# Seven-product pairs with seeded PSUM: two vector additions for five, fixed PSUM regions and mixed values kept in DRAM

## The chip, the cores and the metric

The kernel runs on one NeuronCore of one Trainium2 chip. The metric is the time of one execution in microseconds (us) of the device. In the profile PE is the matmul engine (PEld its weight loads), DVE the vector engine, ACT the scalar (activation) engine, POOL the general one, and SP the engine that issues DMAs (SPq is its queue). SBUF is the core's working memory, PSUM the memory that matmuls write and accumulate in; a PSUM bank holds 512 fp32 values in each of 128 partitions.

## What is computed

One layer of a decoder trunk for 1,032 tokens (a prompt of 1,024 and 8 samples of one token), all of width 1,024:

```python
xn = rmsnorm(h, pre_g)
u, v, z_a, x_b, z_b, g_a, g_b = split(xn @ w_in)              # seven blocks of 1024 columns
u, vn = gelu(u), layernorm(gelu(v), ln_g, ln_b)
y_a = u * (tril(w_s) @ vn + b_s) * silu(z_a)                  # w_s within chunks of 128 tokens
y_b = (pool(x_b) @ blockdiag(w_pool)) * scale * silu(z_b)     # trailing windows 2, 4, 8, 16
m = sigmoid(g_a) * (y_a @ w_pa) + sigmoid(g_b) * (y_b @ w_pb)
h = h + rmsnorm(m @ w_out, post_g)
h = h + rmsnorm(sigmoid(rmsnorm(h) @ w_pg) * (p @ w_ple), ple_out_g)
```

Besides `h` the kernel returns the last chunk's `vn` and the last rows of `x_b`.

## The kernel before, in words

**Seven products for eight.** Each of the large matmuls is split into 2 x 2 blocks and done with seven block products, P1 to P7, in place of eight (the scheme of Strassen in Winograd's form). It works on a *pair*: two blocks of 128 output features at a time (`pairs_of`, four pairs to a block of 1,024). The output of a pair is features first: 128 partitions are features, the columns are tokens, 512 in the first half and 520 (`WIDE`: 512 and the 8 samples) in the second. So the products are narrow (512 columns) or wide (520, as two matmuls of 260). fp32 values are cut into a high and a low part of a rounded type (names ending in `h` and `l`), and three terms (high x high, high x low, low x high) are added up in PSUM: a narrow product is 12 matmuls of 512 columns, a wide one 24 of 260 (`product`).

**Operands.** The 1,024 x 1,032 activations lie in `big`. `Operand.combine` turns their quarters, in place, into the sums B11, B21, B22, T1 to T4 that the products need, and `Operand.cut` cuts each into high and low parts (`xB11h`, `xT3l`, ...), which are kept for all pairs of a stage. On the weights' side `Weights` fetches a pair's 1,024 x 256 raw weights (`gbraw`: two DMAs of 512 KB), forms sums (`gbs`) on DVE, rounds (`gbw`) on ACT, and takes the low part on DVE, all pair by pair.

**A pair's products** (`strassen`, L691). Order P1, P6, P2, P7, P5, P4, P3 (the planner below may move neighbours). `Step` holds for each product what prepares its weights, the matmuls, and `evacuate`, what is done when PSUM holds the result. ACT copies P1 from PSUM to `u` in SBUF (L706, and 8 zero columns from `none`); then DVE makes five additions that read PSUM: u = P6 + u, u7 = P7 + u, and P5 + u7, P4 + u7 and P3 + u, which go to the output tile (`user.summed`). P2 accumulates on P1's bank and is handed on directly (`user.direct`). `User` and its children (`V`, `Gate`, `U`, `ZA`, `XB`, `ZB`, `Merge`, `MergeB`) apply gelu, silu or sigmoid and multiply. The first three v pairs, `EDGES`, have an order of their own (`EDGE`).

**Stages.** Start: loads, transposes of x (`x_half`, PSUM tiles `pst`), the embedding p @ w_ple (`embed`, PSUM tiles `e`), norms, and the first v pairs, interleaved by a list, `SCRIPT`. Then the pairs of v, g_a, u with z_a, x_b with z_b (and after each the pooled matmul, `mixes`), g_b, w_pa, w_pb; then w_out and the gate w_pg, which work tokens first (`strassen_within`), with norms in between, and the outputs. The spatial mixing (`spatial`, L1118) writes its result into `big`, and `ZA.done` (L1198) reads it there. The sums of the windows (`XB.window`) use `big` as scratch as well, each block of a pair its own two rows of it.

**What sets the order.** Nothing is issued as the code stands. Every call goes to a `Planner` (L99), which records operations with a due time from a cost model of its own, and plays them engine by engine from one line (L374, so that every operation of the profile bears that line). `PUSH` moves due times forward (or back, where it is negative) by kind. It also hands out 46 slots of SBUF (`SLOTS`) and, of the three PSUM regions `acc` of two banks each, whichever is free (`region`, L425), under names `pst`, `acc`, `accm`, `acct`, `e`; two more banks serve `bank`. An engine takes its instructions strictly in the order so written, and an instruction waits for its inputs and for its output's place.

Of the kernel before, what the change touches and what calls it, by code (L numbers as in the profile page):

```python
# [14 lines left out]
P = 128  # L15
# [16 lines left out]
PUSH = {'hs': -4.0, 'norm': -5.0, 'half': 0.0, 'cut': -1.0, 'e': 2.0, 'we': -2.0, 'vw': -9.0, 'p': 3.0}  # L32
# [8 lines left out]
OS, GS = 5, 12  # L41
WINDOWS = (2, 4, 8, 16)
# [339 lines left out]
def hybrid_step(  # L382
# [12 lines left out]
    accp = ctx.enter_context(tc.tile_pool(name="accp", bufs=3, space=bass.MemoryType.PSUM))  # L395
    bankp = ctx.enter_context(tc.tile_pool(name="bankp", bufs=2, space=bass.MemoryType.PSUM))
    plan = Planner(nc, SLOTS, {"acc": 3, "bank": 2})
# [64 lines left out]
    big = cpool.tile([P, NB, T], F32, tag="big", name="big")  # L462

# [35 lines left out]
    class Operand:  # L499
# [5 lines left out]
                    "T1": (0, 1), "T2": (0, 0), "T3": (1, 1), "T4": (1, 0)}  # L505
# [9 lines left out]
        def cut(self, what):  # L515
            i, j = self.QUARTERS[what]
            for kk in range(2):
                hi, lo = self.new(what, kk)
                if what == "T2":
                    split(quarter(kk, 0), hi[:, :, :HALF], lo[:, :, :HALF])  # L520
                    split(quarter(2 + kk, 1)[:, :, HALF:], hi[:, :, HALF:], lo[:, :, HALF:])
                else:
                    split(quarter(2 * i + kk, j), hi, lo)

        def combine(self, what):
            for kk in range(2):
                b11, b12, b21, b22 = (quarter(2 * i + kk, j) for i in range(2) for j in range(2))
                if what == "T3":
                    sub(b22, b22, b12)
                elif what == "T1":  # L530
                    sub(b12[:, :, :HALF], b12[:, :, :HALF], b11)
                elif what == "T2":
                    add(b11, b22[:, :, :HALF], b11)
                else:
                    sub(b21, b21, b11)
# [80 lines left out]
    class Features:  # L616

        new = staticmethod(lambda: region("acc"))
# [16 lines left out]
    class Tokens:  # L635

        new = staticmethod(lambda: region("acct")[:, 0])
# [53 lines left out]
    def strassen(weights, operand, user, form=Features, order=None):  # L691
# [41 lines left out]
        for p, a, b, r in sorted(plan, key=lambda x: order.index(x[0])) if order else plan:  # L733
            def run(p=p, a=a, b=b, r=r):
                new = r not in at
                if new:
                    at[r] = form.new()
                product(form, at[r], weights.ready[a], operand, b, new, True, not new)

            steps.append(Step(lambda a=a: weights.prepare(a), run, lambda p=p: evacuate(p)))  # L740
        steps[0].loads = lambda: (weights.fetch(), user.loads())
# [223 lines left out]
    def x_half(j, kps):  # L965

        for kp in kps:
            two = region("pst") if kp != 1 else None
            ps = [bank("pst") if two is None else two[:, kk] for kk in range(2)]
            for i in range(4):  # L970
                plan.apart()
                for kk in range(2):
                    k = 2 * kp + kk
                    nc.tensor.transpose(ps[kk][:, i * P : (i + 1) * P],
                                        xts[4 * j + i][:, k * P : (k + 1) * P], ident)
            out = quarter(kp, j)[:, :, :HALF]
            for kk in range(2):
                o, i, gain = out[:, kk], ps[kk], col(0, 2 * kp + kk)
                if SIDES[4 * j + kp]:
                    nc.scalar.activation(out=o, in_=i, func=AF.Copy, scale=gain)  # L980
                else:
                    nc.vector.tensor_scalar_mul(o, i, gain)
# [22 lines left out]
    vtok = lambda t: sv if t == S else big[:, t, :D]  # L1005
# [112 lines left out]
    def spatial(t):  # L1118

        vh, vl = lnv.pop(("cut", t))  # L1120
        for h2 in range(0, NB, 2):
            ps = bank("mix").rearrange("p (h c t) -> p h c t", h=2, c=2)
            for i in range(2):
                h = h2 + i
                w = lnt["wst"][h // 4][:, h % 4]
                c = slice(h * P, (h + 1) * P)
                nc.tensor.matmul(ps[:, i], vh[:, c], w, start=True, stop=False)
                nc.tensor.matmul(ps[:, i, 0], vl[:, c], w[:, 0], start=False, stop=True)
            o = big[:, t, h2 * P : (h2 + 2) * P].rearrange("p (h t) -> p h t", h=2)
            nc.scalar.activation(out=o, in_=ps[:, :, 0], func=AF.Copy)  # L1130
            add(o, ps[:, :, 1], o)

# [17 lines left out]
    kept["h"] = dram.tile([T, D], F32, tag="h", name="h")  # L1150
    kept["e"] = dram.tile([T, D], F32, tag="e", name="e")
# [68 lines left out]
    def pool_state():  # L1220
        dma(big[: NS * POOL_BUF, 7, :D], state.rearrange("b r d -> (b r) d"))
# [11 lines left out]
    state_sb, tail = big[:, 7, :D], big[:, 6, :D]  # L1233
# [11 lines left out]
    class XB(User):  # L1245
# [10 lines left out]
        def window(self, i):  # L1256
# [4 lines left out]
            s, free = x, [big[:, 2 * i, :], big[:, 2 * i + 1, :]]  # L1261
# [23 lines left out]
    def mixes(g):  # L1285
# [12 lines left out]
        for m in range(2):  # L1298
            def run(m=m):
                for j in range(2):  # L1300
                    ps = held[m, j] = region("accm")
# [55 lines left out]
    for i, (w, u) in enumerate(pairs_of(V0, V, "v")):  # L1357
        vsteps.append(strassen(w, xop, u, order=EDGE if i < EDGES else None))
        vusers.append(u)
    gasteps = [strassen(w, xop, u) for w, u in pairs_of(GA0, Gate, "ga")]  # L1360
    usteps = []
    zausers = []
    for (w, u), (wz, z) in zip(pairs_of(U0, U, "u"), pairs_of(ZA0, ZA, "za")):
        usteps.append((strassen(w, xop, u), strassen(wz, xop, z)))
        zausers.append(z)
    bsteps, xusers = [], []
    for g, ((w, u), (wz, z)) in enumerate(zip(pairs_of(XB0, XB, "xb"), pairs_of(ZB0, ZB, "zb"))):
        bsteps.append((strassen(w, xop, u), strassen(wz, xop, z), mixes(g)))
        xusers.append(u)
    gbsteps = [strassen(w, xop, u) for w, u in pairs_of(GB0, Gate, "gb")]  # L1370

    flat, c = big.rearrange("p b t -> p (b t)"), [T + 4 * w for w in (0, HALF, HALF + WIDE, HALF + 2 * WIDE)]
# [4 lines left out]
    pasteps = [strassen(Weights(merged(w_pa, i), "pa"), yaop, u)  # L1377
               for i, u in enumerate(pausers)]
    pbusers = [MergeB(i, "gb") for i in range(NPAIR)]
    pbsteps = [strassen(Weights(merged(w_pb, i), "pb"), ybop, u)  # L1380
# [6 lines left out]
    for g, (x, z, mix) in enumerate(bsteps):  # L1387
        steps += x[:3] + late + x[3:] + z
        late = mix
    steps += gbsteps[0][:3] + late + gbsteps[0][3:]  # L1390
# [26 lines left out]
    for g, u in enumerate(xusers):  # L1417
# [3 lines left out]
        follow = bsteps[g + 1][0] if g + 1 < NPAIR else gbsteps[0]  # L1421
# [7 lines left out]
        at(follow[5], store)  # L1429
# [9 lines left out]
    PARTS = ("B11", "T2", "B21", "T3", "T4", "T1", "B22")  # L1439
# [257 lines left out]
    def embed(q, n):  # L1697

        hi, lo = pcut[q // 2]
        ps = e_ps[q, n] = region("e")  # L1700
# [28 lines left out]
    def begin():  # L1729
# [68 lines left out]
        def combines():  # L1798
            for what in ("T3", "T1", "T2"):
                xop.combine(what)  # L1800
            xop.cut("T2")
            xop.combine("T4")
            for what in ("T3", "T1", "T4"):
# [58 lines left out]
```

## Time and profile before

| | |
|---|---|
| time, three runs | 976.70, 977.16, 977.18 us (median 977.16) |
| span of the profiled execution | 975.6 us; the median of the runs is 1.6 us above it |
| PE, PEld, DVE, ACT, POOL busy | 963.1, 855.9, 813.4, 497.9, 74.2 us |
| matmuls | 6,037 records |
| moved by SP's queue | 177.43 MB |
| granted clock of PE, mean | 0.998 |

A row of the timeline gives start and duration in us, the engine, the line, the operation, output<-input by the names of the program without their numbers, and shapes as partitions x columns; `x4` is four in a row, and a bracket tells how long the engine had been idle before and what ended that. A row of a group gives busy us and the mean in ns behind the first bar, idle time before it behind the second. A row of waits reads: who <- for whom: us in total, times, longest.

### The profile page before, as it was taken

How to read it: one execution, taken by the hardware profiler on the slowest of the kernel's cores; microseconds unless marked ns; L12 is line 12 of the kernel's file. 1: busy time of each engine (PE TensorE's matmuls, PEld its weight loads, DVE VectorE, ACT ScalarE, POOL GpSimd, SP SyncE). 2: the span in 40 equal slices, each digit the busy share in tenths (PEclk: the TensorE clock that was granted, in tenths of full speed). 3: DMA queues.
4: the chain of work that ended last, by engine and by line, in shares of the span. 5: the costliest groups of instructions: out<-in, count | busy, mean ns of one | idle time of the engine just before them, and what ended most of it. 6: DMA issues, size and time to landing. Idle time of an engine off the chain costs nothing. (4 is left out here: it accounts for less than half of the span.)

```text
span 975.6 us, 15918 instructions
## 1 busy us (share of the span) xinstructions
PE 963.1 (99%) x6037; PEld 855.9 (88%) x6037; DVE 813.4 (83%) x1261; ACT 497.9 (51%) x852; POOL 74.2 (8%) x117
## 2 busy tenths in 40 slices
PE   8999999999999999999999999999999999999996
PEld 6789899999999999999999999999999997788775
DVE  6998568988889788868698897698699899779987
ACT  7664345766444443242434343563263274698655
POOL 2200000000000000000010100000000001323212
PEclk9999999999999999999999999999999999999999
DMA  9523955423467464453425366692492385799896
GB/s 327 172 105 68 192 124 183 155 97 119 164 226 261 136 203 160 140 195 120 152 99 183 134 214 238 228 384 89 158 382 92 111 301 189 151 299 313 224 320 215
DMA packets 128506, 185.82 MB, mean 190 GB/s; under 512 B 42150, under 2 KB 85198, under 8 KB 128421
## 3 DMA queue, kind: packets, MB, share of 16 engines
q1 hardware_dynamic: 126381, 177.43, 54.9%
q0 software_dynamic: 2048, 7.37, 4.1%
q8 instruction: 47, 0.77, 0.3%
q14 instruction: 30, 0.25, 0.1%
HBM read 129.27 MB, written 55.96 MB: 190 GB/s over the span
## 5 line engine op out<-in xcount | busy, mean ns | idle before, releaser
L374 DVE TENSOR_TENSOR u<-acc,u 128x520 f32<-128x520 f32 (+1 forms) x89 | 62.0, 696 | 35.5 <-PE acc L374 35.2
L374 POOL TENSOR_TENSOR rstd<-ms,mhalf 128x1 f32<-128x1 f32 (+1 forms) x37 | 30.9, 841 | 520.3 <-DVE ms L374 517.7
L374 ACT ACTIVATE u<-acc 128x512 f32<-128x512 f32 (+1 forms) x43 | 25.6, 596 | 44.2 <-PE acc L374 44.0
L374 DVE TENSOR_TENSOR big<-big 128x1024 f32<-128x1024 f32 (+4 forms) x20 | 23.8, 1219 | 0.0
L374 POOL COPY big<-xb 128x1 f32<-128x1 f32 x8 | 3.4, 419 | 260.4 <-ACT xb L374 219.7
L374 ACT ACTIVATE paw<-pas 128x512 fp32r<-128x512 f32 x16 | 10.0, 630 | 24.0 <-DVE pas L374 18.2
L374 ACT ACTIVATE pbw<-pbs 128x512 fp32r<-128x512 f32 x16 | 10.0, 628 | 22.1 <-DVE pbs L374 16.8
L374 PE MATMUL accm<-qh,wpoolw 128*128 128x260 f32 (+1 forms) x96 | 20.9, 319 | 0.0
L374 ACT ACTIVATE big<-mix 128x256 f32<-128x256 f32 x32 | 12.0, 382 | 17.1 <-PE mix L374 16.4
L374 ACT ACTIVATE gbw<-gbs 128x512 fp32r<-128x512 f32 x16 | 10.1, 630 | 19.3 <-DVE gbs L374 10.0
L374 DVE SCALAR_TENSOR_TENSOR zb<-accm,gvec,zb 128x512 f32<-128x512 f32 (+1 forms) x16 | 12.0, 754 | 9.4 <-PE accm L374 9.2
L374 ACT ACTIVATE zaw<-zas 128x512 fp32r<-128x512 f32 x16 | 10.0, 628 | 18.1 <-DVE zas L374 10.0
L374 ACT ACTIVATE junk<-h 128x512 bf16<-128x512 f32 x25 | 15.7, 628 | 3.4 <-DVE h L374 2.9
L374 PEld LDWEIGHTS accm<-qh,wpoolw 128*128 128x128 f32 x96 | 15.6, 188 | 1.9
L374 ACT ACTIVATE zbw<-zbs 128x512 fp32r<-128x512 f32 x16 | 10.1, 628 | 13.8 <-DVE zbs L374 8.2
L374 ACT ACTIVATE u<-acct 128x512 f32<-128x512 f32 x22 | 13.0, 589 | 7.4 <-PE acct L374 4.6
L374 DVE TENSOR_TENSOR paw<-pas,paw 128x512 fp32r<-128x512 f32 x16 | 10.9, 688 | 6.7 <-ACT paw L374 6.7
L374 ACT ACTIVATE mw<-ms 128x512 fp32r<-128x512 f32 x16 | 10.0, 625 | 12.4 <-DVE ms L374 9.7
L374 ACT ACT_TABLE_LOAD x11 | 14.1, 1283 | 4.0 <-PE acc L374 2.3
L374 ACT ACTIVATE zbw<-zbraw 128x512 fp32r<-128x512 f32 x12 | 7.5, 623 | 16.6 <-DMA zbraw<-in_w_in_dram 10.7
L374 ACT ACTIVATE gbw<-gbraw 128x512 fp32r<-128x512 f32 x12 | 7.4, 624 | 16.4 <-DMA gbraw<-in_w_in_dram 14.3
L374 PE MATMUL mix<-wst,vh 128*128 128x256 f32 x64 | 15.5, 320 | 0.0
(655 smaller groups left out, 3560.5 us busy)
## 6 DMA issues: line engine op xcount, KB each, us to landing
ga<-ga SPq DMA_DIRECT2D x16, 516.0 KB, 4.6
gb<-gb SPq DMA_DIRECT2D x16, 516.0 KB, 6.2
ya<-za SPq DMA_DIRECT2D x8, 516.0 KB, 3.6
yb<-zb SPq DMA_DIRECT2D x8, 516.0 KB, 4.5
x<-in_x_prompt_dram SPq DMA_DIRECT2D x8, 512.0 KB, 9.3
vraw<-in_w_in_dram SPq DMA_DIRECT2D x8, 512.0 KB, 6.4
e<-e SPq DMA_DIRECT2D x8, 512.0 KB, 3.6
vturned<-v SPq DMA_DIRECT2D x32, 128.0 KB, 4.5
```

What stands on the lines that cost most here:

```text
L374: getattr(getattr(self.nc, e), method)(*(self.real(a) for a in args), **{k: self.real(a) for k, a in kwargs.items()})
```

## The change

`seeded` takes the place of `strassen` for all features-first pairs but the first three of v (33 pairs: one of v, four each of g_a, w_pa, w_pb, g_b, and 16 of u, z_a, x_b, z_b). The sums T1 to T4 of the operand's quarters are the same, but are formed in another order and lie in other places of `big` (T2 = B22 - T1 over B12, T3 = T2 - B11 over B11, B22 stays). The order is P1, P7, P6, P2, P5, P4, P3. ACT copies P1 into the PSUM region in which P6 will be accumulated (the seed, 260 and 252 columns, and the 8 zeros), and P7 to `w` in SBUF. P6 accumulates on the seed. DVE adds `w` to that into the other bank of the first region (`four`, again 260 and 252 columns). P5 accumulates on P6's result, and DVE's second addition adds `w` to it for the output; P4 accumulates on `four`, P3 on the region of P5; both are handed on directly.

The three regions are now fixed tiles (`acc_72`, `acc_73`, `acc_74` in the order of instructions): in a pair the first holds P1, P2 and `four` with its two banks changing places from pair to pair, the second the seed, the third P7. Elsewhere they are taken in turn. The mixed values of a token block go through one of four buffers to DRAM (`kept["mix"]`, eight stores of 512 KB) and come back block by block of features (`mixed`, eight loads of 512 KB). The windows share two scratch rows. A pooled matmul is placed behind all seven products of the next pair (`LATE`) in place of three, with one of its two halves in a bank of `bank`. `PUSH['out']` = 2.0 makes the evacuations of `seeded` due 2 us earlier in the planner's eyes. The matmuls are the same in number and shape. DVE has 1,195 operations in place of 1,261, ACT 852 in place of 757, SP 465 DMAs in place of 449.

```diff
-    plan = Planner(nc, SLOTS, {"acc": 3, "bank": 2})
+    plan = Planner(nc, SLOTS, {"bank": 2})
...
-    def region(name):
-
-        n_name[0] += 1
-        return plan.tile(accp.tile([P, 2, 512], F32, tag="acc", name=f"{name}_{n_name[0]}"), "acc")
+    acc = [plan.tile(accp.tile([P, 2, 512], F32, tag=f"acc{i}", name=f"acc{i}"), "acc") for i in range(3)]
+    turn = [0, 0]
+
+    def region():
+
+        turn[0] += 1
+        return acc[turn[0] % 3]
...
                 b11, b12, b21, b22 = (quarter(2 * i + kk, j) for i in range(2) for j in range(2))
-                if what == "T3":
-                    sub(b22, b22, b12)
-                elif what == "T1":
+                if what == "T1":
                     sub(b12[:, :, :HALF], b12[:, :, :HALF], b11)
                 elif what == "T2":
-                    add(b11, b22[:, :, :HALF], b11)
+                    sub(b12, b22, b12)
+                elif what == "T4":
+                    sub(b21, b21, b12[:, :, :HALF])
                 else:
-                    sub(b21, b21, b11)
+                    sub(b11, b12[:, :, :HALF], b11)
...
+    def seeded(weights, operand, user):
+
+        steps, at, cut = [], {}, (slice(0, QT), slice(QT, HALF))
+        plan_of = (("P1", "A11", "B11"), ("P7", "S3", "T3"), ("P6", "S2", "T2"), ("P2", "A12", "B21"),
+                   ("P5", "S1", "T1"), ("P4", "A22", "T4"), ("P3", "S4", "B22"))
+
+        def evacuate(p):
+            one, four, two, seven = at["r1"], at["r4"], at["r2"], at["r3"]
+            if p == "P1":
+                for q, c in enumerate(cut):
+                    nc.scalar.activation(out=two[:, q, : c.stop - c.start], in_=one[:, c], func=AF.Copy)
+                nc.scalar.activation(out=two[:, 1, HALF - QT : QT], in_=none, func=AF.Copy)
+            elif p == "P7":
+                at["w"] = slot("w", (P, WIDE))
+                nc.scalar.activation(out=Features.like(at["w"]), in_=Features.view(seven, True), func=AF.Copy)
+            elif p == "P6":
+                for q, c in enumerate(cut):
+                    add(four[:, c], two[:, q, : c.stop - c.start], at["w"][:, c])
+            elif p == "P2":
+                user.direct(0, 0, one)
+            elif p == "P5":
+                w = Features.like(at["w"])
+                user.summed(1, 1, Features.view(two, True), w, w)
+            elif p == "P4":
+                user.direct(1, 0, four)
+            elif p == "P3":
+                user.direct(0, 1, Features.view(two, True))
+
+        for p, a, b in plan_of:
+            def run(p=p, a=a, b=b):
+                if p == "P1":
+                    turn[1] ^= 1
+                    at.update(r1=acc[0][:, turn[1]], r4=acc[0][:, 1 - turn[1]], r2=acc[1], r3=acc[2])
+                r = {"P1": "r1", "P2": "r1", "P4": "r4", "P7": "r3"}.get(p, "r2")
+                new = p in ("P1", "P7")
+                product(Tokens if r in ("r1", "r4") else Features, at[r], weights.ready[a], operand, b,
+                        new, True, not new)
+
+            steps.append(Step(lambda a=a: weights.prepare(a), run, lambda p=p: pushed("out", evacuate, p)))
...
-            o = big[:, t, h2 * P : (h2 + 2) * P].rearrange("p (h t) -> p h t", h=2)
+            o = vtok(t)[:, h2 * P : (h2 + 2) * P].rearrange("p (h t) -> p h t", h=2)
...
+        dma(kept["mix"][:, t * P : (t + 1) * P].rearrange("(h p) t -> p h t", p=P),
+            vtok(t).rearrange("p (h t) -> p h t", h=NB))
...
-                zt, mixed = z[:, :SEQ].rearrange("p (t c) -> p t c", c=P), big[:, :, b * P : (b + 1) * P]
+                mixed = slot("mixed", (P, SEQ))
+                dma(mixed, kept["mix"][b * P : (b + 1) * P, :])
...
-    gasteps = [strassen(w, xop, u) for w, u in pairs_of(GA0, Gate, "ga")]
+    gasteps = [seeded(w, xop, u) for w, u in pairs_of(GA0, Gate, "ga")]
...
-        steps += x[:3] + late + x[3:] + z
+        steps += x[:LATE] + late + x[LATE:] + z
```

Three places of the new order follow. The first is ACT within the second pair of g_b: `u` is P1's copy, `gbw` weights, `gb` outputs. Before:

```order
L374 ACTIVATE u_6435<-none 128x8
L374 ACTIVATE gbw_6443<-gbs_6411 128x512
L374 ACTIVATE gb_6402<-gb_6402 128x1032
L374 ACTIVATE u_6435<-acc_431 128x512
L374 ACTIVATE gbw_6482<-gbs_6389 128x512
L374 ACTIVATE gb_6296<-gb_6296 128x520
L374 ACTIVATE gbw_6526<-gbraw_6460 128x512
L374 ACTIVATE gb_6549<-acc_431 128x512
L374 ACTIVATE gbw_6571<-gbraw_6485 128x512
```

In the changed kernel, ACT in the same pair, from the seed's zeros on (`acc_73` is the seed's region, `acc_72` P1's and P2's, `acc_74` P7's):

```order
L375 ACTIVATE acc_73<-none 128x8
L375 ACTIVATE gbw_6313<-gbs_6202 128x512
L375 ACTIVATE acc_73<-acc_72 128x260
L375 ACTIVATE acc_73<-acc_72 128x252
L375 ACTIVATE gbw_6340<-gbraw_6290 128x512
L375 ACTIVATE w_6356<-acc_74 128x520
L375 ACTIVATE gbw_6371<-gbs_6362 128x512
L375 ACTIVATE gb_6411<-acc_72 128x512
L375 ACTIVATE gbw_6423<-gbs_6407 128x512
```

One copy of P1 has become two into PSUM, the copy of P7 has come in, and the rounding of a raw weight of the next pair stands between the seed's copies and P7's.

The second place is the start, PE and DVE, where the last transposes of x meet the fourth v pair's first product. PE before (`pst` transposes, `e` the embedding):

```order
L374 MATMUL pst_172<-ident,x_677 128x128 x2
L374 MATMUL pst_172<-ident,x_679 128x128 x2
L374 MATMUL pst_172<-ident,x_681 128x128 x2
L374 MATMUL pst_172<-ident,x_683 128x128 x2
L374 MATMUL acc_173<-xB11h_838,vw_960 128x512 x4
L374 MATMUL acc_173<-xB11l_857,vw_960 128x512 x2
L374 MATMUL acc_173<-xB11h_851,vw_960 128x512 x4
L374 MATMUL e_174<-wehi_710,ph_915 128x512
```

PE in the changed kernel:

```order
L375 MATMUL acc_72<-ident,x_453 128x128 x2
L375 MATMUL acc_73<-xB11h_614,vw_735 128x512 x4
L375 MATMUL acc_72<-ident,x_455 128x128 x2
L375 MATMUL acc_72<-ident,x_457 128x128 x2
L375 MATMUL acc_72<-ident,x_459 128x128 x2
L375 MATMUL acc_73<-xB11l_633,vw_735 128x512 x2
L375 MATMUL acc_73<-xB11h_627,vw_735 128x512 x4
L375 MATMUL acc_74<-wehi_486,ph_692 128x512
```

DVE at that place before, the copies of the transposes to `big` and the first combines:

```order
L374 TENSOR_SCALAR big<-pst_168,gvec 128x512 x2
L374 TENSOR_SCALAR big<-pst_171,gvec 128x512 x2
L374 TENSOR_SCALAR big<-pst_172,gvec 128x512 x2
L374 TENSOR_TENSOR vw_1019<-vs_1009,vw_1019 128x512
L374 TENSOR_TENSOR xB22l_1057<-big,xB22h_1044 128x1040
```

DVE in the changed kernel:

```order
L375 TENSOR_SCALAR big<-acc_73,gvec 128x512 x2
L375 TENSOR_TENSOR big<-big 128x2x512
L375 TENSOR_SCALAR big<-acc_74,gvec 128x512 x2
L375 TENSOR_SCALAR big<-acc_72,gvec 128x512 x2
L375 TENSOR_TENSOR big<-big 128x2x512
```

The last transposes and the product `xB11` have changed places in part, the embedding's matmul follows in another region, and a combine stands between the copies of DVE.

The third place is the end, ACT and SP. `ge` is a block of gate x embedding, `junk` the squares of a block whose sum is kept. ACT before:

```order
L374 ACTIVATE junk,ssq_631<-ge_10085 128x512
L374 ACTIVATE ge_10065<-ge_10065,hscales 128x512
L374 ACTIVATE ge_10085<-acct_628,hscales 128x256
L374 ACTIVATE junk,ssq_632<-ge_10065 128x512
L374 ACTIVATE ge_10085<-acct_628,hscales 128x256
L374 ACTIVATE junk,ssq_636<-ge_10085 128x256
L374 ACTIVATE junk,ssq_638<-ge_10085 128x256
```

ACT in the changed kernel:

```order
L375 ACTIVATE junk,ssq_407<-ge_9915 128x512
L375 ACTIVATE ge_9890<-ge_9890,hscales 128x512
L375 ACTIVATE ge_9915<-acc_72,hscales 128x256 x2
L375 ACTIVATE junk,ssq_408<-ge_9890 128x512
L375 ACTIVATE junk,ssq_412<-ge_9915 128x256
L375 ACTIVATE junk,ssq_414<-ge_9915 128x256
```

SP's last outputs before (rows of 1,024 fp32 values are 512 KB in 128 partitions):

```order
L374 DMA out_dram<-ge_9918 128x1024
L374 DMA out_dram<-ge_10036 8x512
L374 DMA out_dram<-ge_9907 128x1024
L374 DMA out_dram<-ge_10065 128x512 x2
L374 DMA out_dram<-ge_10085 128x512 x2
```

SP in the changed kernel:

```order
L375 DMA out_dram<-ge_9750 128x1024
L375 DMA out_dram<-ge_9841 8x512
L375 DMA out_dram<-ge_9890 128x512 x2
L375 DMA out_dram<-ge_9915 128x512
L375 DMA out_dram<-ge_9733 128x1024
L375 DMA out_dram<-ge_9915 128x512
```

The squares of 512 columns stand behind both halves of the last block, and an output of 512 KB stands ahead of the last 256 KB.

More of the change, by code (lines that the diff above doesn't have):

```diff
@@ L31 @@
 WE = 1
-PUSH = {'hs': -4.0, 'norm': -5.0, 'half': 0.0, 'cut': -1.0, 'e': 2.0, 'we': -2.0, 'vw': -9.0, 'p': 3.0}
+PUSH = {'hs': -4.0, 'norm': -5.0, 'half': 0.0, 'cut': -1.0, 'e': 2.0, 'we': -2.0, 'vw': -9.0, 'p': 3.0, 'out': 2.0}
 WARM = 9
@@ L616, in hybrid_step @@
     class Features:
-        new = staticmethod(lambda: region("acc"))
+        new = staticmethod(region)
         sums = (P, 2, WIDE)
@@ L635, in hybrid_step @@
     class Tokens:
-        new = staticmethod(lambda: region("acct")[:, 0])
+        new = staticmethod(lambda: region()[:, 0])
         view = staticmethod(lambda ps, wide: ps)
@@ L967, in x_half @@
         for kp in kps:
-            two = region("pst") if kp != 1 else None
+            two = region() if kp != 1 else None
             ps = [bank("pst") if two is None else two[:, kk] for kk in range(2)]
@@ L1260, in window @@
             x = self.out[i]
-            s, free = x, [big[:, 2 * i, :], big[:, 2 * i + 1, :]]
+            s, free = x, [flat[:, KEPT + n * T : KEPT + (n + 1) * T] for n in range(2)]
             for lev in range(levels):
@@ L1300, in run @@
                 for j in range(2):
-                    ps = held[m, j] = region("accm")
+                    plan.apart()
+                    ps = held[m, j] = acc[2 - m] if j else bank("accm").rearrange("p (a t) -> p a t", a=1)
                     c = slice(m * P, (m + 1) * P)
```

54 lines of the change are left out of this document (31 added, 23 removed).

## The prediction

> **What bounds the kernel now.** I read the page's shares first, then the slices of the span, then the waits of PE, then busy time by stretch.
>
> ```profile
> span 975.6 us, 15918 instructions
> PE 963.1 (99%) x6037; PEld 855.9 (88%) x6037; DVE 813.4 (83%) x1261; ACT 497.9 (51%) x852; POOL 74.2 (8%) x117
> PE   8999999999999999999999999999999999999996
> PEclk9999999999999999999999999999999999999999
> ```
>
> PE is full in every slice but the first and the last, at an undiminished granted clock; DVE has 17% free, ACT half. The next view adds up, for the whole span, what PE waited for.
>
> ```profile
> PE warm L374 <- DVE heat L374: 1.5, 1, 1.5
> PE e L374 <- ACT wehi L374: 1.2, 1, 1.2
> PE pst L374 <- DVE big L374: 0.7, 1, 0.7
> PE acct L374 <- ACT ge L374: 0.6, 1, 0.6
> PE acc L374 <- DVE big L374: 0.3, 1, 0.3
> ```
>
> Five waits, 4.3 us together. What ended them are tiles of the start (`heat`, `wehi`, `big`) and the last block's `ge`; none is a `u` or a weight of the pairs. By stretch (columns: length, then busy us and instructions of PE, PEld, DVE, ACT, POOL, the clock, the DMA share and GB/s) it is as plain:
>
> ```profile
> 62.00:250.00 188.00, 188.00 (x1314) 175.00 (x1315) 147.76 (x253) 107.17 (x192) 7.60 (x10) 1.00 0.48 128
> 250.00:800.00 550.00, 550.00 (x3658) 506.19 (x3657) 461.38 (x679) 230.80 (x359) 11.84 (x20) 1.00 0.55 190
> ```
>
> From 62 to 800 us, where nearly every pair is worked that the change rewrites, PE is busy for 738.00 of 738 us. An addition saved on DVE there ends no wait of PE.
>
> **The five additions that become two.** The matmuls are the same in number and shape, in another order, so PE's 963.1 us stay. The additions are priced by this row:
>
> ```profile
> L374 DVE TENSOR_TENSOR u<-acc,u 128x520 f32<-128x520 f32 (+1 forms) x89 | 62.0, 696 | 35.5 <-PE acc L374 35.2
> L374 ACT ACTIVATE u<-acc 128x512 f32<-128x512 f32 (+1 forms) x43 | 25.6, 596 | 44.2 <-PE acc L374 44.0
> L374 ACT ACTIVATE big<-mix 128x256 f32<-128x256 f32 x32 | 12.0, 382 | 17.1 <-PE mix L374 16.4
> ```
>
> Three additions at 0.70 us less in each of 33 pairs, and one of the two left is split (two pieces for one, about 0.1 more): some 66 us less on DVE. ACT copies P1 in two pieces of about 256 columns (0.38 each by the third row) where it copied once (0.60), and P7 besides (0.60): 33 x 0.76, some 25 us more. Neither is on the path that sets the end, because PE has no wait there: the term is 0. What it would cost if that cover went depends on deadlines. Rows of one pair give them (start, duration, engine, what):
>
> ```profile
> 576.28 0.40 PE L374 MATMUL acc<-xT1h,gbw 128*128 128x260 f32 x2
> 579.15 0.40 PE L374 MATMUL acc<-xB11h,gbw 128*128 128x512 f32 x1
> 579.35 0.70 DVE L374 TENSOR_TENSOR gb<-acc,u 128x520 f32<-128x520 f32 x1
> 580.09 1.07 ACT L374 ACTIVATE gb<-gb 128x1032 f32<-128x1032 f32 x1
> 581.94 0.41 PE L374 MATMUL acc<-xB22h,gbw 128*128 128x260 f32 x2
> ```
>
> A wide product (24 matmuls of 260 columns, `xT1`) lasts 576.28 to 579.15, 2.87 us; a narrow one (12 of 512, `xB11`) to 581.94, 2.79 us; a reader on another engine starts 0.20 us after a product ends. *Seeds:* P1 ends, P7 runs 2.87 us, and P6 must find both copies: 0.20 + at worst an activation just begun (1.07) + 0.38 + 0.38 = 2.0, so 0.8 us are to spare. *four:* it must be written within P2's 2.79 us after P6: 0.20 + an addition just begun (0.70) + two pieces of about 0.38 (I price them like ACT's, between 0.35, half the 520-column addition, and 0.70) = 1.7, 1.1 to spare. P5's addition (0.70) has P4's 2.79 us, P4's reading P3's 2.87. The old order had a deadline of the same kind: P1's copy had to leave its bank within P6, and no row shows a wait for it. So I take 0 for all three; the bounds are 0 and the second rival's price. Nothing below 0: there is no wait to end.
>
> **Fixed PSUM regions and the start.** Taken in turn, the regions fall otherwise among the transposes, the embedding and the first v products. In the first trace this place reads:
>
> ```profile
> 37.91 4.07 DVE L374 TENSOR_SCALAR big<-pst,gvec 128x512 f32<-128x512 f32 x6 [0.21 <-PE pst L374]
> 39.46 1.06 PE L374 MATMUL pst<-ident,x 128*128 128x128 f32 x8 [0.72 <-DVE big L374]
> 40.78 1.16 PE L374 MATMUL acc<-xB11h,vw 128*128 128x512 f32 x4 [0.25 <-DVE big L374]
> 43.18 0.39 PE L374 MATMUL e<-wehi,ph 128*128 128x512 f32 x1
> ```
>
> PE waits 0.72 us for DVE's second copy (37.91 + 2 x 0.68 = 39.27, 0.19 later PE goes on) and 0.25 for its fourth. By the new order the last transposes need a region whose reader is done, `xB11` needs the one that DVE's first two copies free (so 39.46 again, now with only 2 of these 8 transposes behind it), and `e` the one that the copies after the new combine free (one combine of 1,024 columns ahead, 1.2 us, then two of 0.68: about 41.9). From 39.46: four `xB11` matmuls, 0.93 at 0.232 us each; six transposes, 6 x 0.13 = 0.8; six more, 1.39: `e` at 42.6 instead of 43.18. **Term: -0.6 us** (bounds -1.0, both waits gone, and -0.3). The other combines of operand quarters come in a new order as well; no row prices a product that would wait for them but these two waits of 0.72 and 0.25, so 0 to 1.0, and I take 0, because PE has the embedding's matmuls to go on with there.
>
> **Mixed values through DRAM.** Eight stores and eight loads of 512 KB more on SP's queue, 8.4 MB on 177. The nearest transfers:
>
> ```profile
> q1 hardware_dynamic: 126381, 177.43, 54.9%
> e<-e SPq DMA_DIRECT2D x8, 512.0 KB, 3.6
> gb<-gb SPq DMA_DIRECT2D x16, 516.0 KB, 6.2
> ```
>
> A load takes 3.6 to 6.2 us beside products of a pair that last 20 us, in a stretch where the DMA share is 0.55. What stands behind it on SP is other loads and stores of the same stage. Term 0, bounds 0 and 1 us (one late weight). The later mixes and the shared scratch of the pool windows lie on DVE with its free share: 0.
>
> **The end.** This is the place where the new order costs. The old one, first the end of PE by the chain of work that ended last (start, length, what), then the others by the timeline:
>
> ```profile
> 966.20 1.35 PE acct L374 x9
> ```
>
> ```profile
> 965.68 0.47 ACT L374 ACTIVATE ge<-acct,hscales 128x256 f32<-128x256 f32 x1 [0.32 <-PE acct L374]
> 966.49 0.63 ACT L374 ACTIVATE junk<-ge 128x512 bf16<-128x512 f32 x1 [0.34 <-DVE ge L374]
> 967.25 0.21 DVE L374 TENSOR_SCALAR ms<-ssq,sofar 128x1 f32<-128x1 f32 x1 [0.51 <-ACT junk L374]
> 967.38 0.68 DVE L374 TENSOR_TENSOR ge<-ge,out 128x512 f32<-128x512 f32 x1
> 967.58 0.47 ACT L374 ACTIVATE ge<-acct,hscales 128x256 f32<-128x256 f32 x1 [0.36 <-PE acct L374]
> 967.95 0.41 ACT L374 ACTIVATE junk<-ge 128x256 bf16<-128x256 f32 x1
> 969.73 0.41 DVE L374 TENSOR_TENSOR ge<-ge,out 128x256 f32<-128x256 f32 x1
> 970.07 2.07 DVE L374 SCALAR_TENSOR_TENSOR ge<-ge,rstd,hback 128x512 f32<-128x512 f32 x3
> ```
>
> ACT squares the last but one block (512 columns) between the two halves of the last block, while PE still works. By the new order both `ge` of the last block come first; the squaring waits behind the second of them, which PE lets start at 967.58, and starts 0.37 later (as the row at 967.95 does), 967.95 instead of 966.49. `ms` follows 0.76 later, as from 966.49 to 967.25: 968.71. Then DVE has `ms`, a 512-column product, `sofar`, a 256, `ms`, a 256 (0.13 for the small ones as from 967.25 to 967.38, 0.34 for a 256 as from 969.73 to 970.07, some 0.60 for the 512): 968.71 + 0.13 + 0.60 + 0.13 + 0.34 + 0.13 + 0.34 = 970.38, and four last operations of 0.69, where before three were left: 973.1 instead of 972.14, **+1.0 us**. On SP an output of 512 KB, which before stood ahead of all these pieces, stands ahead of the very last 256 KB:
>
> ```profile
> 966.00:970.00 4.00, 1.34 (x9) 1.14 (x9) 3.46 (x10) 2.25 (x8) 1.03 (x2) 1.00 0.90 362
> 972.00:974.00 2.00, 0.00 (x0) 0.00 (x0) 0.14 (x1) 0.00 (x0) 0.00 (x0) 0.50 0.89 333
> ```
>
> ```profile
> out_dram<-ge SPq DMA_DIRECT2D x4, 256.0 KB, 2.1
> ```
>
> 333 / 0.89 = 374 GB/s and 362 / 0.90 = 402 while the queue is busy, so 524 KB take 1.3 to 1.4 us. It waits on SP for the third of the last operations and goes out some 0.7 us ahead of the last, so 0.6 to 1.4 us of it lie before the last transfer: **+0.9 us**. Together +1.9 (bounds +0.6, if only a part of the late squaring shows, and +2.4).
>
> [...]
>
> **The sum.** The profiled execution's span is 975.6 us; the median of the runs, 977.16, lies 1.6 us above it, and I take that as unchanged. 975.6 - 0.6 + 0 + 0 + 1.9 = 976.9, so 977.16 + 1.3 = 978.5 us. A measurement of this kernel can tell about 0.2% from no change, that is 2 us: 975.2 to 979.1 is "the same".
>
> **The rivals.**
>
> *The tail doesn't lengthen.* If the late squaring hides behind other work and SP's long output has left before, only the start's gain is left and perhaps DVE's +1.0: 976.2 to 977.6. For it: the ends are 0.4 us apart on several engines. Against it: ACT and SP take their rows in order, and the rows stand as said.
>
> *A copy waits behind a raw weight.* ACT also takes its work in order, and in the new order the first rounding of a raw weight stands between the seed copies and P7's copy to `w`. The first trace shows what such a rounding can wait for:
>
> ```profile
> ACT gbw L374 <- DMA gbraw<-in_w_in_dram: 14.3, 4, 7.0
> ACT zbw L374 <- DMA zbraw<-in_w_in_dram: 10.7, 4, 7.7
> ```
>
> Eight waits, 25.0 us in all, the longest 7.0 and 7.7, with no wait of PE behind them today. `w` is due late in P2, before `four`: from the seeds' end (about 1.0 us into P7) there are 1.9 + 2.87 + 2.79 us, less 0.60 for `w`, 0.76 for `four` and 0.4 for two hand-overs: 5.8 us. It decides from there on: waits of 7.0 and 7.7 would stop PE for 1.2 and 1.9 us, 3.1 together, and 978.5 becomes 981.6, slower. For it: the planner's costs for landings are as rough as before, and 8.4 MB more share the queue. Against it: the six other waits are 10.3 us in all, and DVE's lighter load frees weight slots, and so starts loads, earlier. PE would show idle time <-DVE or <-ACT at a `xT1` or `xT4` product of the zb or gb pairs.
>
> *PE gains after all.* With fewer readers in PSUM the matmuls could follow each other more closely: 0.5% of 738 us would be 3.7 us, 975 us. Nothing for it in the rows: DVE is busy for 0.79 of the first stretch above and 0.84 of the second, and PE is full in both.
>
> *The change does nothing at all* (DVE's and ACT's loads move, PE never knew): 977.2; it is the first rival without the start's gain, and counted there.
>
> **How the numbers follow.** Cover holds and the tail lengthens: 0.56, at 978.5, between 977.0 and 979.6, of which 0.45 within 0.2% and 0.11 above. The tail doesn't lengthen: 0.12, all within. A copy behind a raw weight: 0.26, 979.5 to 984, slower. A blocked transfer of the mixed values: 0.02, slower. PE gains: 0.04, faster. So faster 0.04, same 0.57, slower 0.39. Range: 976.2, the start's gain alone, to 982.0, both long waits unhidden; some 0.06 lie below, 0.12 above.
>
> **What would show it.** Right: PE busy 963 us with the same two small waits gone or halved near 39 us; DVE near 750 us, ACT near 525; the squaring (`junk`, 512 columns) after both 256-column `ge`, and a span that ends 8.6 to 10.4 us after the last matmul instead of the 8.0 of before (975.6 less 966.20 + 1.35). Wrong: waits of PE for an `acc` that ACT or DVE writes, between 62 and 800 us; or a last matmul that ends more than 1.5 us before 967.5.

## The result and the profile after

The changed kernel takes 1036.18 us (median of four runs, 1034.89 to 1037.01), the kernel before 977.17 beside it: 1.0587 times as long, 95% interval 1.0573 to 1.0601. The forecast was 978.5 with a range up to 982.0. It was wrong by 58 us, on the slow side.

The first lines of the page of the changed kernel:

```profile
span 1035.0 us, 16036 instructions
PE 983.7 (95%) x6037; PEld 854.1 (83%) x6037; DVE 761.7 (74%) x1195; ACT 528.2 (51%) x947; POOL 73.4 (7%) x117
PEclk9999999999999999999999999999999999999998
```

DVE is relieved by 52 us and ACT loaded by 30 (66 and 25 were forecast), and PE has the same 6,037 matmuls at nearly the same granted clock (0.994 on the mean, 0.998 before). But PE is no longer full. Its waits over the whole span:

```profile
PE acc L375 <- DVE acc L375: 34.4, 64, 0.7
PE acc L375 <- ACT u L375: 2.7, 2, 2.2
...
PE acc L375 <- ACT ge L375: 0.7, 1, 0.7
```

64 waits for an `acc` that DVE writes: about two in each of 33 pairs. Four places in the program tell in which stage the 59.4 us of the span came. The first two are the first transposition of the spatial weights, a little past the start, and the first matmul of w_out with `woT3`, when all pairs are done. (`woB11`, which opens w_out, will not do: it stands ahead of the last product of the last pair in the kernel before, and behind it in the changed one.) Before:

```profile
79.27 0.38 PE L374 MATMUL psw<-ident,ws 128*128 128x128 f32 x2
...
803.08 0.40 PE L374 MATMUL acct<-woT3h,mw 128*128 128x512 f32 x1
```

and in the changed kernel:

```profile
78.62 0.38 PE L375 MATMUL psw<-ident,ws 128*128 128x128 f32 x2
...
854.77 0.39 PE L375 MATMUL acc<-woT3h,mw 128*128 128x512 f32 x1
```

and the last matmuls of the changed kernel, in its chain of work that ended last:

```profile
1023.38 1.34 PE acc L375 x9
```

Up to the first place 0.65 us are won. From there to the second the kernel before takes 803.08 - 79.27 = 723.81 us, the changed one 854.77 - 78.62 = 776.15: **52.3 us lost while the pairs are worked**. From the second to the end of the last matmul it is 164.5 us before and 170.0 after, 5.5 lost; and from there to the end of the span 8.0 before and 10.3 after, 2.2 lost. -0.65 + 52.3 + 5.5 + 2.2 = 59.4.

What happens in each pair is seen in the first pair of g_b. P2 (`xB21`) begins; P6 has just ended; the two rows `acc<-acc,w` of DVE are the pieces of `four`:

```profile
597.36 0.39 PE L375 MATMUL acc<-xB21h,gbw 128*128 128x512 f32 x1
597.59 0.40 PE L375 MATMUL acc<-xB21l,gbw 128*128 128x512 f32 x1
598.21 0.43 DVE L375 TENSOR_TENSOR acc<-acc,w 128x260 f32<-128x260 f32 x1
598.69 0.49 PE L375 MATMUL acc<-xB21h,gbw 128*128 128x512 f32 x1 [0.70 <-DVE acc L375]
599.23 0.43 DVE L375 TENSOR_TENSOR acc<-acc,w 128x252 f32<-128x252 f32 x1 [0.59 <-PE acc L375]
599.71 0.50 PE L375 MATMUL acc<-xB21h,gbw 128*128 128x512 f32 x1 [0.52 <-DVE acc L375]
600.04 0.39 PE L375 MATMUL acc<-xB21l,gbw 128*128 128x512 f32 x1
```

Read it from the top: two matmuls of P2, then PE stops until DVE has written the first piece; one matmul; DVE's second piece has stood still for 0.59 us *waiting for PE*, namely for that one matmul; PE stops again for the second piece. The two engines hand the region to and fro. Yet P2 writes one bank of the first region and `four` the other, and no value goes from one to the other in either direction. The built program has the waits in it, in the order with its semaphores (the same product in the next pair, and the two pieces of `four` in an earlier one):

```
L375 MATMUL acc_72<-xB21h_680,gbw_6249 128x512 [waits DVE_49] x2
...
L375 TENSOR_TENSOR acc_72<-acc_73,w_1523 128x260 [waits PE_49,Activation_49]
L375 TENSOR_TENSOR acc_72<-acc_73,w_1523 128x252 [waits PE_49]
```

Both banks are one tile, `acc[0]`, and the program that is built from the planner's order makes these writes of a tile wait for the write of another engine to the same tile that stands ahead of them. The planner compares columns and so sees two independent operations; it lays matmuls and pieces one between the other, by time. P2's first two matmuls come 597.59 - 597.36 = 0.23 us apart; the next ones come 598.69 - 597.59 = 1.10 and 599.71 - 598.69 = 1.02 apart, and then once 600.04 - 599.71 = 0.33: 0.87 + 0.79 + 0.10 = 1.76 us lost in this pair, one of the dearest. Added up over the 33 pairs, it is 91.85 us from P2's first matmul to that of the next product before, and 143.20 in the changed kernel: 51.35 us more, 1.56 in a pair. That is nearly all of the 52.3. (The row of waits says only 34.4, because the profile counts PE as busy to the modelled end of a matmul, 0.4 to 0.5 us, and not to the 0.23 at which the next one followed in the first two rows. Distances between starts give the loss.)

This is theory A. The rivals I set against it: B, `four` comes late through DVE's or ACT's queue; C, other parts of the change cost the time. The expectations below reckon with 1.67 us in every pair, 55 in all, where the sum over the pairs is 51.

### The profile page after: what moved, and what is told of

It reads as the page before. It is cut to its first block, busy times and chain, and to the rows that moved or that the text cites. A ratio compares the mean times of both kernels' runs of the same rounds, so it can differ in the third digit from the quotient of the medians.

```text
span 1035.0 us, 16036 instructions
## 1 busy us (share of the span) xinstructions
PE 983.7 (95%) x6037; PEld 854.1 (83%) x6037; DVE 761.7 (74%) x1195; ACT 528.2 (51%) x947; POOL 73.4 (7%) x117
## 5 line engine op out<-in xcount | busy, mean ns | idle before, releaser
L375 DVE TENSOR_TENSOR acc<-acc,w 128x260 f32<-128x260 f32 x66 | 28.5, 432 | 60.8 <-PE acc L375 60.5
L375 ACT ACTIVATE acc<-acc 128x260 f32<-128x260 f32 x66 | 24.3, 369 | 38.9 <-PE acc L375 37.8
L375 ACT ACTIVATE w<-acc 128x520 f32<-128x520 f32 x33 | 19.9, 603 | 32.3 <-PE acc L375 32.3
L375 ACT ACTIVATE acc<-none 128x8 f32<-128x8 f32 x33 | 5.9, 180 | 27.0 <-DVE zb L375 10.3
L375 ACT ACTIVATE xbw<-xbs 128x512 fp32r<-128x512 f32 x16 | 10.1, 628 | 18.2 <-DVE xbs L375 16.7
L375 ACT ACTIVATE uw<-us 128x512 fp32r<-128x512 f32 x16 | 10.0, 628 | 16.5 <-DVE us L375 9.5
L375 ACT ACTIVATE gb<-acc 128x512 f32<-128x512 f32 (+1 forms) x12 | 7.2, 601 | 21.5 <-PE acc L375 21.4
L375 ACT ACTIVATE xb<-acc 128x512 f32<-128x512 f32 (+1 forms) x12 | 7.2, 597 | 20.7 <-PE acc L375 20.7
L375 DVE TENSOR_TENSOR gbw<-gbs,gbw 128x512 fp32r<-128x512 f32 x16 | 10.9, 688 | 9.2 <-ACT gbw L375 9.1
L375 ACT ACTIVATE zb<-acc 128x512 f32<-128x512 f32 (+1 forms) x12 | 7.2, 602 | 19.6 <-PE acc L375 19.5
L375 PE MATMUL acc<-xB21h,gbw 128*128 128x512 f32 x32 | 12.1, 418 | 4.4 <-DVE acc L375 4.4
```

Of the source, the lines that this page charges most:

```text
L375: getattr(getattr(self.nc, e), method)(*(self.real(a) for a in args), **{k: self.real(a) for k, a in kwargs.items()})
```

## The experiments

Times are medians in us beside the kernel before on the same chip (978.7 to 979.0 there); kernels without an interval were run once.

### e1 and e3: `four` in another region, and in more pieces there

```diff
-                    at.update(r1=acc[0][:, turn[1]], r4=acc[0][:, 1 - turn[1]], r2=acc[1], r3=acc[2])
+                    at.update(r1=acc[0][:, turn[1]], r4=acc[2][:, 0], r2=acc[1], r3=acc[2])
```

> Edit: `four` is written to the first bank of the third region (P7's, read by ACT's copy to `w` just before) and no longer to the other bank of the region in which P2 is accumulated; P4 then accumulates there. Nothing is left out. Theory A (P2 and `four` lie in two banks of one tile, so each of the two pieces of `four` waits for the matmul of P2 ahead of it, and the next matmul of P2 waits for the piece): the two waits of PE in each P2 vanish, 33 x about 1.67 = 55 us go, time 977 to 982 us, DVE's and ACT's busy time unchanged within 3 us. Theory B (DVE or ACT is late with `four`, through its queue or the wait for `w`): the waits move to P5 or P4, time above 1015 us. Theory C (the rest of the change, fixed regions, DRAM or order, costs the time): above 1020 us.

982.51 us against 978.80, 1.0033 (1.0022 to 1.0044). No wait of PE for DVE's `acc` is left, and the 33 P2 take 91.85 us in all, as before the change; DVE is busy 759.7 us and ACT 528.7, as in the changed kernel. So neither engine was late (B), and the other parts (C) are worth 2 to 4 us here. The expectation needs one correction, for something is left out: in e1 part of the sum that P4 and `four` make together does not reach the output. P7 fills only 260 columns of that bank and `four` has 512; that the loss lies in the other 252 is my reading, and no trace shows it. Matmuls and additions are the same in number and size. e5 leaves nothing out.

The same place with four pieces, the edit of e2 below on top of this one:

> Edit: both edits together, `four` in four pieces, and in the third region. Nothing is left out. Theory A: without the shared tile the number of pieces costs nothing on PE, the time of e1 within 2 us. Theory B: longer than e1 by 10 us or more, since `four` ends later.

985.29 us in one run, 2.8 above e1's median and within e1's own 980.74 to 987.0. That is 0.8 more than the 2 us of the expectation, and one run can't tell it from e1. The same part of the sum is left out. PE has no wait for DVE's `acc` in this kernel either: in a region that no product fills at that time, the four pieces stopped nothing.

### e2: four pieces in the shared tile

```diff
-                    add(four[:, c], two[:, q, : c.stop - c.start], at["w"][:, c])
+                    for d in (slice(0, 130), slice(130, c.stop - c.start)):
+                        e = slice(c.start + d.start, c.start + d.stop)
+                        add(four[:, e], two[:, q, d], at["w"][:, e])
```

> Edit: the changed kernel, but `four` is added in four pieces (130, 130, 130 and 122 columns) in place of two. Nothing is left out. Theory A: each piece stops PE once within P2, so four waits in place of two; at about 0.6 us for a piece of half the width (0.76 for the whole one) 4 x 0.6 in place of 2 x 0.8 in 33 pairs, some 26 us more: 1055 to 1070 us, and about 130 waits of PE for DVE `acc` in place of 64. Theory B: the additions end at nearly the same time, 1033 to 1042 us, and the number of waits stays near 64.

1094.19 us: 58 more than with two pieces, twice what theory A had put down and beyond its range, with 111 waits of PE for DVE's `acc` (about 130 expected); B is out. One pair of w_pa of this kernel, P2's stops and what follows them, and then the stretches of four and three us there (length, busy time of PE and the other engines, the clock):

```profile
729.85 0.49 PE L375 MATMUL acc<-yaB21h,paw 128*128 128x512 f32 x1 [0.73 <-DVE acc L375]
730.74 0.50 PE L375 MATMUL acc<-yaB21l,paw 128*128 128x512 f32 x1 [0.39 <-DVE acc L375]
731.62 1.06 PE L375 MATMUL acc<-yaB21h,paw 128*128 128x512 f32 x2 [0.39 <-DVE acc L375]
732.48 0.63 PE L375 MATMUL acc<-yaB21l,paw 128*128 128x512 f32 x1
732.91 1.05 PE L375 MATMUL acc<-yaB21h,paw 128*128 128x512 f32 x2
```

```profile
728.00:732.00 4.00, 2.49 (x10) 1.35 (x9) 2.03 (x6) 2.94 (x4) 0.00 (x0) 0.98 0.96 340
732.00:735.00 3.00, 3.00 (x9) 2.36 (x8) 1.97 (x3) 0.00 (x0) 0.00 (x0) 0.50 0.89 306
```

Here the first stop holds two pieces and the others one each. In a stop the next matmul comes 0.89 us after the last in place of 0.23, 0.66 lost; with the longer first one 2.2 us in this pair, and 2.5 in pairs with four stops. Over all pairs the gaps of more than 0.6 us within P2 lose 76.9 us by this count, in the changed kernel 46.9: 30 more, near the 26 of theory A. The other half of the 58 is the clock, which theory A had not foreseen: *after* the stops the matmuls come 0.43 apart for three us at a granted clock of 0.50. The trace has 19 such stretches between 138 and 903 us, and the mean clock of the span is 0.966, where it is 0.994 in the changed kernel; the 28 us that are left make 1.5 for each.

### e5: a bank of its own

The two banks of `bank` become fixed tiles as well (left out here), and all else that takes a bank has the second of them while the pairs run:

```diff
...
-                    at.update(r1=acc[0][:, turn[1]], r4=acc[0][:, 1 - turn[1]], r2=acc[1], r3=acc[2])
+                    if not spare[1]:
+                        spare[:] = 1, True
+                        plan.apart()
+                        nc.tensor.matmul(banks[0], heat[:, :P], heat, start=True, stop=True)
+                    at.update(r1=acc[0][:, turn[1]], r4=banks[0], r2=acc[1], r3=acc[2])
...
```

> Edit: the changed kernel, but `four` and P4 have a bank of their own (one of the two that served transposes and mixes; while the pairs run, those have the other alone), P1 and P2 stay where they were; one matmul of 512 columns more, which readies that bank. Nothing is left out. Theory A (P2 and `four` in two banks of one tile): no wait of PE for DVE `acc` in P2, 977 to 984 us, as in e1. Theory B (DVE or ACT late): above 1015 us. What a single bank for the mixes costs would show as waits for `mix` or `accm` tiles between 140 and 560 us; I expect less than 3 us.

983.70 against 978.67, 1.0049 (1.0036 to 1.0062). P1, P2 and the seed lie where the change put them, the whole sum is computed, and the loss is gone: PE has no wait for DVE's additions into that bank, the 33 P2 take 92.33 us in all, and from the first place to the second it is 726.60 us, 2.8 more than before the change. Its pieces of `four` are as long as they were:

```profile
L375 DVE TENSOR_TENSOR bank<-acc,w 128x260 f32<-128x260 f32 x33 | 14.3, 434 | 25.7 <-PE acc L375 18.8 <-PE bank L375 6.5 <-ACT wgraw L375 0.3
L375 DVE TENSOR_TENSOR bank<-acc,w 128x252 f32<-128x252 f32 x33 | 14.1, 429 | 1.1
```

### e6: the planner knows of the shared tile

```diff
         return (x[1] < y[2] and y[1] < x[2]
-                and any(a < d and c < b for a, b in x[3] for c, d in y[3]))
+                and (x[0].startswith("acc") and y[0].startswith("acc") or any(a < d and c < b for a, b in x[3] for c, d in y[3])))
```

> Edit: the changed kernel, but the planner treats any two accesses to one of the three regions as touching, as the built program does. Nothing is left out. Theory A: `four` then stands wholly ahead of P2's first matmul, one wait in place of two: P6's end to P2's start 0.20 + 0.43 + 0.38 + 0.05 = 1.1 us in 33 pairs, 36 us above e1: 1013 to 1023 us, about 33 waits of some 1.0 us. Theory B: no change, 1033 to 1040 us.

1015.31 us, 33 above e1 and within theory A's range: same tile, same banks, same pieces, but `four` as a whole ahead of P2, and no stop within P2 (33 of them take 93.87 us). That the time fits is in part luck. Of 33 stops of about 1 us ahead of P2 only 16 came; in the other pairs the planner's new order has other matmuls between P6 and P2, which cover `four`. Nine more stops are for the seed's part (`ACT acc`), which the same order lets come late, ahead of P6:

```profile
PE acc L375 <- DVE acc L375: 15.3, 16, 1.3
PE acc L375 <- ACT acc L375: 9.9, 9, 1.1
```

### e4, e7, e8: what is left over

e4 puts the old function back for all pairs (`strassen` for `seeded` in the lists of steps) and keeps all else of the change.

> Edit: the changed kernel with the old function for the products of all pairs (five additions, P1 copied to SBUF) in place of the new one; fixed regions taken in turn, the new combines, mixed values through DRAM, the later pooled matmul stay. Nothing is left out. Theory A: the 55 us of the P2 waits go, what is left is the start (-0.6) and the end (some +2 to +5): 977 to 983 us. Theory C: above 1000 us.

984.15, 1.0047 (1.0035 to 1.0059): 1.2 above the range. By the intervals of e1, e4 and e5, 2 to 6 us belong to other parts. Theory D: to the regions in turn; E: to the rest. e7 is the kernel before with this one edit (the pool of the three regions is set up to match):

```diff
...
-    def region(name):
-
-        n_name[0] += 1
-        return plan.tile(accp.tile([P, 2, 512], F32, tag="acc", name=f"{name}_{n_name[0]}"), "acc")
+    acc = [plan.tile(accp.tile([P, 2, 512], F32, tag=f"acc{i}", name=f"acc{i}"), "acc") for i in range(3)]
+    turn = [0]
+
+    def region(name):
+
+        turn[0] += 1
+        return acc[turn[0] % 3]
```

> Edit: the kernel before with one part of the change, the three regions fixed and taken in turn in place of the planner's choice of a free one. Nothing is left out. Theory D (the 3 to 5 us that e1 and e4 leave over the kernel before come from regions in turn, in the tokens-first stages): 980 to 984 us, with PE waits for ACT `u` behind 800 us. Theory E (they come from other parts: DRAM for the mixed values, the new combines, the later pooled matmul): 976 to 979 us.

984.68, 1.0058 (1.0045 to 1.0071), 0.7 above theory D's range. And e8, e4 with that edit undone:

> Edit: e4 (the old function for all pairs, the rest of the change) with the planner's choice among three regions as before. Nothing is left out. Theory D: 976 to 979 us. Theory E: 981 to 985 us, as e4.

979.79, 1.0007 (0.9999 to 1.0016), 0.8 above D's range and below E's. D holds on both sides: regions in turn cost 6 us in the kernel before and some 4 in e4 (984.15 less 979.79), and the new combines, the mixed values through DRAM and the later pooled matmul together none that can be told. By the traces' places, e7's span is 7.4 us longer: 0.8 won at the start, 1.6 lost in the pairs, 2.6 in w_out, 1.7 in the gate and 2.2 behind the last matmul. The loss in w_out begins here (DVE and PE), first the same transpose in the kernel before:

```profile
867.92 1.25 DVE L374 STREAM_TRANSPOSE big<-hblocks 128x1024 f32<-128x1024 f32 x1 [0.71 <-DMA hblocks<-h]
```

and e7:

```profile
872.04 1.25 DVE L374 STREAM_TRANSPOSE big<-hblocks 128x1024 f32<-128x1024 f32 x1 [3.07 <-DMA hblocks<-h]
873.21 1.24 DVE L374 SCALAR_TENSOR_TENSOR h<-h,rstd,post 128x1024 f32<-128x1024 f32 x1
874.37 0.69 DVE L374 TENSOR_TENSOR acc<-acc,u 128x512 f32<-128x512 f32 x1
875.75 0.50 PE L374 MATMUL acc<-woT1h,mw 128*128 128x512 f32 x1 [2.08 <-ACT u L374]
```

DVE stands for 3.07 us in place of 0.71 at a transpose whose rows have not come back from DRAM; behind it in its queue is the addition for which PE, by way of ACT's `u`, waits.

### e9 and e10: the reload taken as later

```diff
-            op.lands = 2.0
+            op.lands = 8.0 if 'hblocks' in writes[0].tensor.name else 2.0
```

> Edit: e7 (the kernel before with regions in turn), and the planner takes the reload of the normalised rows (`hblocks`) as landing 6 us later than it did, so that DVE's transposes of them are ordered behind additions that PE waits for. Nothing is left out. Theory F (e7's loss is DVE standing at a transpose whose reload has not landed, with P6's addition of the next product queued behind it): the wait of 2.1 us near 875 us goes, and time falls by 2 to 5 us, to 980 to 982.5 us. Theory G (the regions themselves hold PE up): no change, 984 to 985.5 us.

> Edit: e5 (the changed kernel, `four` and P4 in a bank of their own) with the planner's reload of `hblocks` 6 us later, as in e9. Nothing is left out. Theory F: 1 to 3 us less than e5, 980.5 to 982.5 us. Theory G: as e5, 983 to 984.5 us.

e9 took 985.61 (1.0069, 1.0057 to 1.0082), e10 990.37 (1.0121, 1.0107 to 1.0134): e9 just above theory G's range, e10 6 us above it. The wait near 875 us did go, and the last matmul of e9 ends at 969.2 us where e7's ends at 972.7; but the span is 983.8 for e7's 983.0, so that 14.6 us now follow the last matmul in place of 10.3. What was taken from the waits of PE was given back at the end, where DVE and POOL have norms still to do. e10 has two waits of PE in the gate that e5 does not have:

```profile
PE acc L375 <- ACT hw L375: 3.4, 1, 3.4
PE bank L375 <- DMA wgrow<-wg: 1.5, 1, 1.5
```

Theory F is right on the wait and wrong on the time; that the regions themselves hold PE up (G) is not shown by this either. What in the planner's order of the tokens-first stages costs e7 its 6 us I leave open. No version beat the kernel before: e8 is equal to it.

## Why the prediction was wrong, step by step

**The step that failed** is the one on `four`: "it must be written within P2's 2.79 us after P6 ... 1.1 to spare". Its durations were nearly right (pieces of 0.43 us where I had 0.38), and DVE was in time: in the pair shown the first piece begins 0.85 us after P2's start, behind another addition of 0.69, as the step allowed. The step took P2 for the cover, and P2 is the one product that shares a tile with `four`. The step rested on the *values* not depending on each other and on the *banks* being different ones, and left out the question on which unit the built program waits. The orders quoted ahead of the prediction are without semaphores; with them, the two waits in the middle of P2 can be seen. The profile of before cannot show this, because no pair there writes the two banks of one region from two engines at the same time. As a price it was a term of 0 that measured 51 to 52 us, and e1 and e5, which move `four` out of the tile, take it away. The prediction had named the sign: waits of PE for an `acc` that DVE writes, between 62 and 800 us.

**What held.** No wait of PE was ended by the saved additions, and nothing was gained from 52 us less on DVE. The start: -0.6 forecast, -0.65 measured, and by the rows that were worked out: `xB11` begins at 39.46 us again and the embedding's matmul at 42.55, forecast 42.6. The end: +1.9 forecast, +2.2 measured from the last matmul to the end. Its rows came as worked out, the squares of 512 columns (`junk`) 0.38 us after the second `ge`, and four last operations in place of three:

```profile
1024.74 0.47 ACT L375 ACTIVATE ge<-acc,hscales 128x256 f32<-128x256 f32 x1 [1.42 <-PE acc L375]
1025.12 0.62 ACT L375 ACTIVATE junk<-ge 128x512 bf16<-128x512 f32 x1
1027.50 2.74 DVE L375 SCALAR_TENSOR_TENSOR ge<-ge,rstd,hback 128x512 f32<-128x512 f32 x4
```

DVE ends 5.5 us after the last matmul, where it ended 4.6 after it before: +0.9 of the +1.0 that I had. e7, which has the regions in turn and nothing else of the change, ends in the same way, 10.3 us after its last matmul, so this term comes with them too. The seed's copies took 0.37 us, forecast 0.38, and no P6 waited for them.

**The rivals.** That a copy waits behind a raw weight did not happen: ACT's waits for raw weights of z_b are 3.5 us in all, the longest 2.0, and those for g_b are gone. The blocked transfer of mixed values did not happen either (e8). The one that would have been right, a dependency between operations that need nothing of each other, was not among them.

**What was missed besides.** 5.5 us in the tokens-first stages, 4.4 in w_out and 1.1 in the gate. In the changed kernel PE waits there once for 2.16 us, at the same `woT1h` as in e7, and about 1.1 us after it goes on, the granted clock falls to 0.50 for 3.4 us, as these two pieces of the span show:

```profile
926.87 0.50 PE L375 MATMUL acc<-woT1h,mw 128*128 128x512 f32 x1 [2.16 <-ACT u L375]
```

```profile
924.53:927.94 3.41, 1.25 (x6) 0.89 (x6) 3.41 (x5) 1.91 (x4) 0.92 (x1) 1.00 1.05 388
927.94:931.35 3.41, 3.41 (x10) 2.63 (x9) 3.41 (x5) 3.24 (x4) 0.84 (x1) 0.50 1.07 356
```

I had priced the regions in turn at the start alone, where they brought 0.6 us, and not in the stages behind 800 us, where in e7's trace they cost 2.6 + 1.7 us, and 2.2 at the end.

## What to carry to other kernels

Before two engines are set to work beside each other on parts of one tile, look on which unit the built program waits: read the order with its semaphores for the product that is to be the cover, not only the order. A wait between two instructions of one product was the sign of it here (64 of them), and a place outside that tile took it away (none left in e1 and e5). And where PE was full, the 52 us saved on DVE were worth nothing, while each new hand-over inside a product cost 0.7 to 0.9 us, two of them in each of 33 pairs 51.

## What the runs showed of the hardware

While PE still had work to do, the granted clock fell to 0.50 behind idle times of PE of 2.16 us and less. In e2 no single wait within P2 was above 0.9 us, but three or four stops stood in a row (in the pair shown PE was busy for 2.49 of 4 us), and the clock was 0.50 for the next three us. That came in 19 of the 33 pairs; at 658 us four stops stood in a row, with 2.44 of 4 us busy, at a clock of 1.00. Two waits in a row, as in the changed kernel, had it in no pair (its clock is 1.00 from 62 to 854 us). Of single waits, one of 2.16 us in the changed kernel and one of 1.84 us in e1 were followed by 3.4 us at 0.50, and one of 2.08 us in e7 was not. e2's place at 658 us, and then e1's wait and what came behind it:

```profile
658.00:662.00 4.00, 2.44 (x10) 1.08 (x8) 1.52 (x6) 0.00 (x0) 0.00 (x0) 1.00 0.24 86
```

```profile
963.49 0.50 PE L375 MATMUL acc<-wgT1h,hw 128*128 128x512 f32 x1 [1.84 <-ACT u L375]
963.89:967.31 3.42, 3.42 (x10) 2.67 (x9) 3.31 (x6) 1.66 (x4) 1.73 (x2) 0.50 0.61 111
```

What decides which stops are followed by such a stretch is not shown, and no run was made to test it.
